# Down projections of four feed-forward layers as seven half-size products, woven into the next up projection, with one PSUM pool

## The chip, the cores and the metric

The kernel runs on one NeuronCore of a Trainium2 chip. Its engines work side by side, each through an order of instructions that is fixed when the kernel is built: TensorE (PE) multiplies, VectorE (DVE), ScalarE (ACT) and GpSimd (POOL) do the elementwise work, and SyncE (SP) issues nearly all loads. An engine starts its next instruction when the semaphores that this instruction waits for are up; the ones behind it wait with it. The metric is the device time of one execution in microseconds.

## What is computed

Two transformer blocks of two layers each run over 512 tokens of width 1024, in fp32.

```python
# block one, layers 0 and 1
x = layer_norm(ALPHA * x + mixer(x), ...)            # l=0: HGRN2 recurrence + convolution; l=1: pooling mixer
x = layer_norm(ALPHA * x + memory_cross_attention(x, mem_n, wq, wk, wv, wo), ...)
x = layer_norm(ALPHA * x + swiglu_ffn(x, ffn_wg[l], ffn_wu[l], ffn_wd[l]), ...)
# block two: gated linear attention (layer 0), sliding-window attention (layer 1), and after each
x = x + sq_relu_mlp(rmsnorm(x, g), w_up[l], w_down[l])

def swiglu_ffn(x, w_gate, w_up, w_down):             # hidden width 2816
    return (jax.nn.silu(x @ w_gate) * (x @ w_up)) @ w_down

def sq_relu_mlp(h, w_up, w_down):                    # hidden width 4096
    u = jax.nn.relu(h @ w_up)
    return (u * u) @ w_down
```

## The kernel before

**Products.** A number is held as two fp32r parts, high and low (`split`: ACT writes the high part, line 152, and DVE the rest, line 153). `mm3` (lines 180 to 182) makes one product of three matmuls: high by high, high by low, low by high. Weights come through SP in pieces of 512 KB, two blocks of 128 rows by 512 columns (`chunk`, line 161), into `rawp`, and are split into `wp`.

**Layers.** The 512 tokens are four tiles `r[0]` to `r[3]` of 128 rows. A projection whose output must stand with features on the partitions is `lin_a`; one whose output stands by token is `lin_b`, and the last one of a sublayer is `lin_out`. A feed-forward layer goes through its hidden features in blocks: `ffn` in blocks of 1024, 1024 and 768, `mlp` in four of 1024. Each block first makes the hidden values (with gate and up projection, or with the up projection alone), and then its part of the down projection for all 1024 outputs, which `resid` adds to `r`. The last block's part is a `lin_out`.

**Hand-over between sublayers.** `lin_out` makes the output by halves of 512 columns and by token tiles. When a tile's second half is done, `tail` adds it to `r[t]`, normalises `r[t]` where the layer asks for it (DVE and POOL, lines 275 to 294), and `nxt` makes what the next sublayer needs: `next_split` transposes `r[t]` on TensorE (line 254) and splits the result; `next_unit` first scales `r[t]` by its root mean square (ACT line 454, POOL, ACT line 479, into `z`) and transposes `z`; `next_pool` multiplies with banded matrices. The order in `lin_out` is, as (half, tile):

```python
for half, t in ((0, 0), (0, 1), (1, 0), (1, 1), (0, 2), (0, 3), (1, 2), (1, 3)):
```

**What sets the order.** The program is written sublayer by sublayer. A scheduler builds each engine's order from it when the kernel is built: program order is the priority, weight loads are raised by `high_priority`, and an instruction that is not ready may be passed by later ones. Buffers of one pool and tag are handed out in program order. PSUM has eight banks: five in the pool `mm` (accumulators of projections, `bank`) and three in the pool `aux` (`xbank`: transposes, attention scores, running sums, recurrence states).

Of the kernel before, what the change touches and what calls it, by code (L numbers as in the profile page):

```python
# [21 lines left out]
D_FF = 2816  # L22
# [50 lines left out]
class Net:  # L73
    def __init__(self, tc, a, ctx):
        self.tc, self.nc, self.a = tc, tc.nc, a
        pool = lambda name, bufs, **kw: ctx.enter_context(tc.tile_pool(name=name, bufs=bufs, **kw))
        self.const = pool("const", 1)
        self.wp = pool("wp", 4)
        self.rawp = pool("rawp", 3)
        self.big = pool("big", 16)  # L80
        self.work = pool("work", 2)
        self.small = pool("small", 4)
        self.mm = pool("mm", 5, space=bass.MemoryType.PSUM)
        self.aux = pool("aux", 3, space=bass.MemoryType.PSUM)
# [45 lines left out]
        return bank  # L130

    def xbank(self, shape):
        return self.aux.tile(shape, F32, tag="aux", name=self.nm("aux"))

    def bload(self, dst, ap):
        self.nc.sync.dma_start(dst, ap.unsqueeze(0).broadcast_to(list(dst.shape)))
# [38 lines left out]
                units.append(u)  # L175
        return units

    def mm3(self, ps, lh, ll, rh, rl, start, stop):
        nc = self.nc
        nc.tensor.matmul(ps, lh, rh, start=start, stop=False)  # L180
        nc.tensor.matmul(ps, lh, rl, start=False, stop=False)  # L181
        nc.tensor.matmul(ps, ll, rh, start=False, stop=stop)  # L182

    def lin_a(self, xT, W, c0, evac, w=512, halves=False, width=512, **kw):
        units = kw.pop("units", None) or self.chunk(W, c0, w, **kw)
        nf = w // 128
        spans = [(0, width // 2), (width // 2, width)] if halves else [(0, width)]
        for t0, t1 in spans:
            ps = [self.bank([128, t1 - t0]) for _ in range(nf)]
            for k in range(8):  # L190
                u = units[k // 2]
                xh, xl = xT(k)
                for f in range(nf):
                    sl = slice(f * 128, f * 128 + 128)
                    self.mm3(ps[f], u[:, 0, k % 2, sl], u[:, 1, k % 2, sl],
                             xh[:, t0:t1], xl[:, t0:t1], k == 0, k == 7)
            for f in range(nf):
                evac(f, ps[f], t0, t1)

    def lin_out(self, xT, W, first, norm, nxt, k0=0, nk=8, between=None, aside=None):  # L200
# [12 lines left out]
        nxt, early = nxt if isinstance(nxt, tuple) else (nxt, None)  # L213
        ev = self.tail(512, first, norm, nxt)
        for half, t in ((0, 0), (0, 1), (1, 0), (1, 1), (0, 2), (0, 3), (1, 2), (1, 3)):
            if half == 0:
                p = ps[t] or self.bank([128, 512])
                self.mm_b([p], [t], xT, ua, range(split, nk), nk)
                self.resid(t, p, 0, first)
                if early:  # L220
                    early(t)
            else:
                p = self.bank([128, 512])
                self.mm_b([p], [t], xT, ub, range(nk), nk)
                ev(t, p)
# [67 lines left out]
        else:  # L293
            self.nc.vector.tensor_tensor(r, r, ps, ALU.add)  # L294

# [1 line left out]

    def hgrn_mixer(self):
        nc, a = self.nc, self.a
# [475 lines left out]
    def ffn(self, l, nxt, aside):  # L775
        nc, a = self.nc, self.a
        xT = self.pair_view(self.hi, self.lo)
        lg, lb = self.gains("ln_ffn", l)
        first = True
        for b0, bw in ((0, 1024), (1024, 1024), (2048, 768)):  # L780
            nch = -(-bw // 512)
            hh, hl = self.new_xT("hid", nch)
            for c in range(nch):
                w = min(512, bw - c * 512)
                sg = self.slot([128, 4, 512], name="sg")
                self.lin_a(xT, a["ffn_wg"][l], b0 + c * 512,
                           lambda f, ps, t0, t1: nc.scalar.activation(sg[:, f, t0:t1], ps, AF.Silu),
                           w=w, halves=(first and c == 0))

                def ev_up(f, ps, t0, t1):  # L790
                    s = sg[:, f, t0:t1]
                    nc.vector.tensor_tensor(s, s, ps, ALU.mult)
                    self.split(hh[c][:, f, t0:t1], hl[c][:, f, t0:t1], s)
                self.lin_a(xT, a["ffn_wu"][l], b0 + c * 512, ev_up, w=w)
            hT = self.pair_view(hh, hl)
            last = b0 + bw == D_FF
            kw = dict(k0=b0 // 128, nk=bw // 128)
            f0 = first
            if last:
                self.lin_out(hT, a["ffn_wd"][l], f0, (lg, lb), nxt, aside=aside, **kw)  # L800
            else:
                self.lin_b(hT, a["ffn_wd"][l], 0, lambda t, ps: self.resid(t, ps, 0, f0), **kw)
                self.lin_b(hT, a["ffn_wd"][l], 512, lambda t, ps: self.resid(t, ps, 512, f0), **kw)
            first = False


# [1 line left out]

    def gla_prepare(self):
        nc, a = self.nc, self.a  # L810
# [85 lines left out]
    def mlp(self, l, nxt):  # L896
        nc, a = self.nc, self.a
        xT = self.pair_view(self.hi, self.lo)
        for b in range(4):
            hh, hl = self.new_xT("hid")  # L900
            for c in range(2):
                def ev_up(f, ps, t0, t1):
                    u = self.tmp()[:, :t1 - t0]
                    nc.scalar.activation(u, ps, AF.Relu)
                    nc.vector.tensor_tensor(u, u, u, ALU.mult)
                    self.split(hh[c][:, f, t0:t1], hl[c][:, f, t0:t1], u)
                self.lin_a(xT, a["w_up_2"][l], b * 1024 + c * 512, ev_up, halves=(b == 0 and c == 0),
                           gain=self.gain(2 + l))
            hT = self.pair_view(hh, hl)
            kw = dict(k0=b * 8, nk=8)  # L910
            if b == 3:
                self.lin_out(hT, a["w_down_2"][l], False, None, nxt, **kw)
            else:
                self.lin_b(hT, a["w_down_2"][l], 0, lambda t, ps: self.resid(t, ps, 0), **kw)
                self.lin_b(hT, a["w_down_2"][l], 512, lambda t, ps: self.resid(t, ps, 512), **kw)

    def rel_bias(self):
        nc, a = self.nc, self.a
# [204 lines left out]
```

## Time and profile before

| | |
|---|---|
| time, median of three runs | 2504.81 us (2504.08 to 2505.48) |
| span of the profiled execution | 2503.4 us |
| TensorE busy | 2458.3 us (98%) |
| VectorE busy | 1249.7 us (50%) |
| ScalarE busy | 944.6 us (38%) |
| GpSimd busy | 181.3 us (7%) |
| moved by DMA | 239.48 MB, 96 GB/s on the mean |

The profiled execution's span is 1.4 us below the median of the runs; sums are made on the span. Busy shares are means over the whole span; a stage's own limit is read from its window. The clock that TensorE was granted is shown as PEclk, where 1.00 is 2.4 GHz and 0.50 is 1.2 GHz.

### The profile page before, as it was taken

The page shows a single profiled execution, that of the slowest core. Times are in us where ns is not written, and L with a number is a line of the kernel's source. Part 1 is how long each engine was busy: PE and PEld are TensorE (multiplying, and loading weights), DVE is VectorE, ACT ScalarE, POOL GpSimd, SP SyncE. Part 2 cuts the span into 40 slices and gives each one's busy share as a digit, 9 for nine tenths or more (in the row PEclk, how much of TensorE's full clock was granted, in tenths as well). Part 3 has the DMA queues.
Part 4 walks back from the last instruction along what each step waited for, and adds up shares of the span by engine and source line. Part 5 has one row for each costly group of instructions (what it writes and reads, how often), then busy time and mean ns, then how long its engine had stood idle before and what let it go on. Part 6 is the DMA issues. An engine that isn't in the chain of part 4 may idle for free.

```text
span 2503.4 us, 30298 instructions
## 1 busy us (share of the span) xinstructions
PE 2458.3 (98%) x12334; PEld 2052.4 (82%) x12334; DVE 1249.7 (50%) x1772; ACT 944.6 (38%) x1576; POOL 181.3 (7%) x219
## 2 busy tenths in 40 slices
PE   8989999999999999999999999999999999999998
PEld 8876787888888997888888786888888877888887
DVE  4798566433326766433327423444444467444443
ACT  3643343222223343322224634433223456423323
POOL 1151300000000100000001003100000100000000
PEclk9999899999999999999999999999999999999999
DMA  6323122333324332233223223233222421222222
GB/s 214 109 102 102 53 85 77 92 99 95 99 74 144 123 130 76 85 101 99 95 76 121 69 85 43 76 101 101 93 101 98 142 74 51 72 97 95 99 93 84
DMA packets 121788, 239.48 MB, mean 96 GB/s; under 512 B 7849, under 2 KB 14309, under 8 KB 121392
## 3 DMA queue, kind: packets, MB, share of 16 engines
q1 hardware_dynamic: 118976, 229.73, 28.3%
q0 software_dynamic: 2096, 6.76, 1.4%
q8 instruction: 97, 1.59, 0.3%
q10 hardware_dynamic: 576, 1.05, 0.1%
q14 instruction: 43, 0.35, 0.0%
HBM read 234.34 MB, written 6.32 MB: 96 GB/s over the span
## 4 chain that ended last, share of the span: by engine, by line
PE 90%; DVE 6%; issue 1%; ACT 1%; DMA 1%; POOL 0%; SPq 0%; POOLq 0%; DVEq 0%; ACTq 0%
PE mm L180 28%; PE mm L181 27%; PE mm L182 27%; DVE acc L525 2%; PE aux L254 2%; PE aux L581 1%; DVE w L153 1%; PE aux L180 1%; PE mm L608 1%; PE mm L605 1%; PE aux L182 1%; PE aux L181 1%; DVE bn L275 0%; PE aux L1043 0%; DMA raw<-in_ffn_wg 0%
## 5 line engine op out<-in xcount | busy, mean ns | idle before, releaser
L153 DVE TENSOR_TENSOR w<-raw,w 128x1024 fp32r<-128x1024 f32 (+1 forms) x286 | 341.0, 1195 | 604.4 <-ACT w L152 604.1
L181 PE MATMUL mm<-xTl,w 128*128 128x512 f32 (+1 forms) x1696 | 614.0, 363 | 2.2 <-DVE xTl L153 2.2
L180 PE MATMUL mm<-xTh,w 128*128 128x512 f32 (+1 forms) x1696 | 610.4, 363 | 1.0 <-ACT w L152 0.8
L182 PE MATMUL mm<-xTh,w 128*128 128x512 f32 (+1 forms) x1696 | 605.7, 362 | 0.0
L152 ACT ACTIVATE w<-raw 128x1024 fp32r<-128x1024 f32 (+1 forms) x286 | 293.8, 1029 | 748.8 <-PE mm L182 598.3
L181 PEld LDWEIGHTS mm<-xTl,w 128*128 128x128 f32 x1696 | 321.5, 190 | 50.8 <-DVE xTl L153 2.4
L180 PEld LDWEIGHTS mm<-xTh,w 128*128 128x128 f32 x1696 | 320.9, 190 | 50.4 <-ACT w L152 1.2
L182 PEld LDWEIGHTS mm<-xTh,w 128*128 128x128 f32 x1696 | 319.4, 189 | 48.8
L181 PE MATMUL mm<-w,hidh 128*128 128x512 f32 x752 | 292.0, 389 | 0.0
L180 PE MATMUL mm<-w,hidh 128*128 128x512 f32 x752 | 291.1, 389 | 0.0
L182 PE MATMUL mm<-w,hidl 128*128 128x512 f32 x752 | 288.9, 389 | 0.0
L173 DVE SCALAR_TENSOR_TENSOR w<-raw,gains_T,w 128x512 fp32r<-128x512 f32 (+1 forms) x200 | 139.0, 738 | 212.0 <-ACT w L172 211.3
L172 ACT ACTIVATE w<-raw,gains_T 128x512 fp32r<-128x512 f32 (+1 forms) x200 | 131.3, 707 | 237.3 <-PE mm L182 220.9
L182 PEld LDWEIGHTS mm<-w,hidl 128*128 128x128 f32 x752 | 141.2, 188 | 29.3
L180 PEld LDWEIGHTS mm<-w,hidh 128*128 128x128 f32 x752 | 141.2, 188 | 29.2
L181 PEld LDWEIGHTS mm<-w,hidh 128*128 128x128 f32 x752 | 141.2, 188 | 29.1
L180 PE MATMUL mm<-w,xTh 128*128 128x512 f32 (+1 forms) x352 | 135.1, 386 | 0.0
L181 PE MATMUL mm<-w,xTh 128*128 128x512 f32 (+1 forms) x352 | 135.1, 384 | 0.0
L182 PE MATMUL mm<-w,xTl 128*128 128x512 f32 (+1 forms) x352 | 134.8, 384 | 0.0
L294 DVE TENSOR_TENSOR r<-r,mm 128x512 f32<-128x512 f32 x112 | 76.3, 686 | 72.8 <-PE mm L182 72.7
L525 DVE SCALAR_TENSOR_TENSOR acc<-u,pack,acc 128x511 f32<-128x511 f32 (+29 forms) x90 | 83.7, 972 | 0.0
L180 PEld LDWEIGHTS mm<-w,xTh 128*128 128x128 f32 x352 | 66.5, 189 | 15.5 <-issue 2.3
(323 smaller groups left out, 3344.9 us busy)
## 6 DMA issues: line engine op xcount, KB each, us to landing
raw<-in_w_up SPq DMA_DIRECT2D x64, 512.0 KB, 3.6
raw<-in_w_down SPq DMA_DIRECT2D x64, 512.0 KB, 3.2
raw<-in_ffn_wd SPq DMA_DIRECT2D x44, 512.0 KB, 3.2
raw<-in_ffn_wg SPq DMA_DIRECT2D x40, 512.0 KB, 3.6
raw<-in_ffn_wu SPq DMA_DIRECT2D x40, 512.0 KB, 3.5
raw<-in_ab_w_in SPq DMA_DIRECT2D x24, 512.0 KB, 3.8
raw<-in_a_w_in SPq DMA_DIRECT2D x24, 512.0 KB, 3.6
raw<-in_xa_wk SPq DMA_DIRECT2D x16, 512.0 KB, 3.3
```

The lines of the kernel that those rows point to most:

```text
L152: self.nc.scalar.activation(hi, src, AF.Copy)
L153: self.nc.vector.tensor_tensor(lo, src, hi.bitcast(F32), ALU.subtract)
L172: nc.scalar.activation(u[:, 0, i], raw[:, i], AF.Identity, scale=g)
L173: nc.vector.scalar_tensor_tensor(u[:, 1, i], raw[:, i], g, u[:, 0, i].bitcast(F32), ALU.mult, ALU.subtract)
L180: nc.tensor.matmul(ps, lh, rh, start=start, stop=False)
L181: nc.tensor.matmul(ps, lh, rl, start=False, stop=False)
L182: nc.tensor.matmul(ps, ll, rh, start=False, stop=stop)
L254: self.nc.tensor.transpose(ps[:, j, :], src[:, j * 128:j * 128 + 128], self.ident)
L294: self.nc.vector.tensor_tensor(r, r, ps, ALU.add)
L525: nc.vector.scalar_tensor_tensor(dst, src, col, dst, ALU.mult, ALU.add)
L581: nc.tensor.matmul(d[:, h - h0, :], ke[rows, t, h * 128:h * 128 + 128], vh(t, h)[rows, :], start=True, stop=True)
L605: nc.tensor.matmul(o, P[:, h, :], vh(t, h), start=True, stop=False)
```

## The change

**Down projections.** In each feed-forward layer, the down projection of every block but the last is made by `down_steps`. It cuts a product of 512 tokens by 1024 hidden features by 1024 outputs into halves in all three directions and makes seven products of half size instead of eight, after Strassen and Winograd: sums and differences of the hidden blocks (`s1`, `s2`) and of the weight blocks (`chain`) go into products that share accumulators (`x`, `y`, `z`, two banks each). There are two such blocks in each of two `ffn` layers and three in each of two `mlp` layers, ten in all.

**Order of the work.** `down_steps` and the hidden projections of the next block (`hidden`, `lin_steps`) are generators. `weave` takes one product and then two steps (`ffn`) or one step (`mlp`) of the other in turn.

**Pools.** The two PSUM pools become one of eight banks, `xbank` takes from it too, `rawp` grows from 3 to 5 and `big` shrinks from 16 to 15.

```diff
-        self.rawp = pool("rawp", 3)
-        self.big = pool("big", 16)
+        self.rawp = pool("rawp", 5)
+        self.big = pool("big", 15)
-        self.mm = pool("mm", 5, space=bass.MemoryType.PSUM)
-        self.aux = pool("aux", 3, space=bass.MemoryType.PSUM)
+        self.mm = pool("mm", 8, space=bass.MemoryType.PSUM)
     def xbank(self, shape):
-        return self.aux.tile(shape, F32, tag="aux", name=self.nm("aux"))
+        return self.mm.tile(shape, F32, tag="mm", name=self.nm("aux"))
+    def weave(self, main, side, per):
+        main, side = iter(main), iter(side)
+        for _ in main:
+            for _ in range(per):
+                next(side, None)
+        for _ in side:
+            pass
+    def down_steps(self, h, W, k0, first, ahead=120):
...
+        def product(d, us, banks, start):
+            for t in range(2):
+                tk = slice(t * 128, t * 128 + 128)
+                for k in range(4):
+                    u = us[k // 2]
+                    self.mm3(banks[t], d[:, 0, k, tk], d[:, 1, k, tk], u[:, 0, k % 2], u[:, 1, k % 2],
+                             start and k == 0, k == 3, skip_group_check=not start)
...
+        with early():
+            tt(s1, a21, a22, ALU.add)
+            d = left(s1)
+            us = []
+            for c, p, q in zip(halves(chain), block(0, 1), block(0, 0)):
+                tt(c, p, q, ALU.subtract)
+                us.append(self.wsplit(c))
+        z = pair()
+        product(d, us, z, True)
+        out(1, 1, z)
+        yield
...
     def mlp(self, l, nxt):
...
-            if b == 3:
-                self.lin_out(hT, a["w_down_2"][l], False, None, nxt, **kw)
-            else:
-                self.lin_b(hT, a["w_down_2"][l], 0, lambda t, ps: self.resid(t, ps, 0), **kw)
-                self.lin_b(hT, a["w_down_2"][l], 512, lambda t, ps: self.resid(t, ps, 512), **kw)
+        for b in range(1, 4):
+            more = []
+            out = self.new_xT("hid") if b == 3 else None
+            self.weave(self.down_steps(h, a["w_down_2"][l], 8 * b - 8, False), hidden(b, more, out), 1)
+            h = more
+        self.lin_out(self.pair_view(*out), a["w_down_2"][l], False, None, nxt, k0=24, nk=8)
```

Two places show what becomes of the order of TensorE's instructions. The first is the end of block one's layer 0 cross-attention: `xa_wo`'s second half for token tile 1 (before, its last rows for tile 3), the transposes of `r1` and `r2` (the rows with `consts`, the identity), and the next projection `ffn_wg` (`xTh`, `w`). In the kernel before:

```order
L181 MATMUL mm_485_3614<-wb_462_3405,oh_449_3350 128x512
L182 MATMUL mm_485_3614<-wb_462_3405,ol_450_3351 128x512
L254 MATMUL aux_477_3524<-consts_79,r1_88 128x128 x4
L254 MATMUL aux_478_3531<-consts_79,r1_88 128x128 x4
L254 MATMUL aux_483_3600<-consts_79,r2_110 128x128 x4
L180 MATMUL mm_506_3693<-xTh_463_3408,w_499_3675 128x256
L180 MATMUL mm_507_3694<-xTh_463_3408,w_499_3675 128x256
```

In the changed kernel, where `mm_473` is the second half of tile 1 and `mm_479` that of tile 2:

```order
L180 MATMUL mm_473_3485<-wb_462_3402,oh_449_3347 128x512
L181 MATMUL mm_473_3485<-wb_462_3402,ol_450_3348 128x512
L391 MATMUL aux_477_3521<-consts_76,r1_85 128x128 x4
L391 MATMUL aux_478_3528<-consts_76,r1_85 128x128 x4
L179 MATMUL mm_479_3561<-wb_456_3387,oh_429_3233 128x512
L180 MATMUL mm_479_3561<-wb_456_3387,oh_429_3233 128x512
```

Before, the transposes of tile 1 stood behind the products of all four tiles (`mm_485` is that of tile 3). Now they stand directly behind the product of tile 1, and the product of tile 2 stands behind them; tiles 2 and 3 follow in the same way.

The second place is the end of block one's layer 1: `ffn_wd`'s last block and the transposes of `z`, the scaled `r[0]`, for the gated linear attention. In the kernel before, `mm_1226` is the second half of tile 1, `mm_1235` and `mm_1236` are the first halves of tiles 2 and 3 (36 matmuls), and `mm_1237` is the second half of tile 2:

```order
L182 MATMUL mm_1226_9927<-wb_1207_9814,hidl_1149_9380 128x512
L180 MATMUL mm_1235_9978<-w_1197_9789,hidh_1146_9377 128x512
...
L182 MATMUL mm_1236_9998<-w_1201_9799,hidl_1149_9380 128x512
L180 MATMUL mm_1237_10018<-wb_1203_9804,hidh_1146_9377 128x512
L254 MATMUL aux_1224_9913<-consts_79,z_1222_9907 128x128 x4
L254 MATMUL aux_1225_9920<-consts_79,z_1222_9907 128x128 x4
L181 MATMUL mm_1237_10018<-wb_1203_9804,hidh_1146_9377 128x512
```

In the changed kernel, `mm_1293` is the second half of tile 0 and `mm_1302` that of tile 1:

```order
L180 MATMUL mm_1293_10005<-wb_1283_9943,hidh_1176_9206 128x512
L181 MATMUL mm_1293_10005<-wb_1283_9943,hidl_1178_9208 128x512
L391 MATMUL aux_1300_10042<-consts_76,z_1298_10036 128x128 x4
L391 MATMUL aux_1301_10049<-consts_76,z_1298_10036 128x128 x4
L179 MATMUL mm_1302_10056<-wb_1279_9933,hidh_1175_9205 128x512
L180 MATMUL mm_1302_10056<-wb_1279_9933,hidh_1175_9205 128x512
```

Before, the rest of tile 1 and 37 matmuls of tiles 2 and 3 stood between the end of tile 0's product and the transposes of its `z`; now none does.

## Rows read from the trace of the kernel before

**Rows 1.** The page: the span, and busy time by engine:
```profile
span 2503.4 us, 30298 instructions
...
PE 2458.3 (98%) x12334; PEld 2052.4 (82%) x12334; DVE 1249.7 (50%) x1772; ACT 944.6 (38%) x1576; POOL 181.3 (7%) x219
```

**Rows 2.** The weight loads' issues in SP's queue, start and length in us:
```profile
1672.16 40.11 SPq L161 DMA_DIRECT2D raw<-in_w_up  x8
...
1846.24 0.37 SPq L161 DMA_DIRECT2D raw<-in_w_up  x1
```

**Rows 3.** Busy us of each engine over two middle blocks of the first mlp:
```profile
1672.16:1846.24 174.08, 174.08 (x770) 144.20 (x769) 73.47 (x96) 55.80 (x80) 0.00 (x0) 1.00 0.30 97
```

**Rows 4.** Busy us in the first of nine hand-over windows, and the sum of all nine:
```profile
318.00:334.00 16.00, 13.53 (x100) 13.00 (x99) 11.40 (x16) 3.07 (x6) 3.52 (x4) 0.89 0.38 132
...
sum 317.00, PE 312.19 PEld 269.51 DVE 206.08 ACT 119.00 POOL 46.69; mean PE 34.69 PEld 29.95 DVE 22.90 ACT 13.22 POOL 5.19
```

**Rows 5.** Groups of DVE instructions by line and shape, mean ns of one:
```profile
L153 DVE TENSOR_TENSOR w<-raw,w 128x1024 fp32r<-128x1024 f32 x266 | 327.3, 1233 | 565.9 <-ACT w L152 565.7
...
L294 DVE TENSOR_TENSOR r<-r,mm 128x512 f32<-128x512 f32 x112 | 76.3, 686 | 72.8 <-PE mm L182 72.7
...
L905 DVE TENSOR_TENSOR tmp<-tmp 128x512 f32<-128x512 f32 x56 | 37.9, 691 | 25.3 <-ACT tmp L904 25.3
```

**Rows 6.** DVE in order of time after xa_wo, token tile 0:
```profile
427.16 0.69 DVE L292 SCALAR_TENSOR_TENSOR r<-r,mm 128x512 f32<-128x512 f32 x1 [3.19 <-PE mm L182]
427.88 0.69 DVE L275 BATCH_NORM_STATS2 bn<-r 128x6 f32<-128x512 f32 x1
428.61 0.21 DVE L277 BATCH_NORM_AGGREGATE mv<-bn 128x2 f32<-128x12 f32 x1
428.86 1.28 DVE L286 SCALAR_TENSOR_TENSOR r<-r,mv,w4k 128x1024 f32<-128x1024 f32 x1
430.92 1.29 DVE L287 SCALAR_TENSOR_TENSOR r<-r,rs,w4k 128x1024 f32<-128x1024 f32 x1 [0.78 <-POOL rs L269]
```

**Rows 7.** ACT in order of time after a_w_out_2, token tile 0:
```profile
1585.46 1.06 ACT L454 ACTIVATE z<-r 128x1024 f32<-128x1024 f32 x1 [5.16 <-DVE r L294]
1586.43 0.19 ACT L454 ACTIVATION_READ_ACCUMULATOR z<-r 128x1 f32 x1
1587.56 1.15 ACT L479 ACTIVATE z<-r,rs 128x1024 f32<-128x1024 f32 x1 [0.95 <-POOL rs L269]
```

**Rows 8.** POOL in order of time before a_w_out_2:
```profile
1559.63 4.82 POOL L885 TENSOR_TENSOR g<-g,w4k 128x512 f32<-128x512 f32 x3 [0.62 <-ACT g L883]
```

**Rows 9.** Busy us and clock (PEclk) in TensorE gaps and behind them:
```profile
128.50:131.80 3.30, 0.00 (x0) 0.00 (x0) 3.30 (x5) 1.24 (x2) 1.95 (x1) 1.00 0.17 40
131.90:136.00 4.10, 4.10 (x11) 3.21 (x12) 4.10 (x6) 0.22 (x2) 1.57 (x1) 0.58 0.23 86
141.20:144.20 3.00, 0.00 (x0) 0.00 (x0) 3.00 (x5) 1.08 (x2) 1.74 (x2) 1.00 0.19 72
144.30:152.00 7.70, 7.70 (x51) 7.70 (x52) 7.70 (x13) 2.55 (x3) 1.69 (x2) 0.78 0.20 69
195.98:197.56 1.58, 0.00 (x1) 0.00 (x0) 1.58 (x3) 1.06 (x1) 0.00 (x0) 1.00 0.00 0
197.60:201.70 4.10, 4.10 (x22) 3.16 (x22) 4.10 (x6) 0.00 (x0) 0.00 (x0) 1.00 0.48 135
320.20:322.40 2.20, 0.00 (x0) 0.00 (x0) 2.20 (x4) 0.00 (x0) 0.00 (x0) 1.00 0.68 238
322.40:330.00 7.60, 7.60 (x51) 7.60 (x52) 5.02 (x6) 0.58 (x2) 1.88 (x2) 0.78 0.26 93
2037.15:2039.10 1.95, 0.00 (x0) 0.02 (x1) 1.95 (x3) 0.93 (x2) 0.00 (x0) 1.00 0.00 0
2039.10:2047.00 7.90, 7.76 (x27) 5.81 (x28) 6.16 (x11) 2.67 (x9) 0.00 (x0) 0.57 0.22 69
```

More of the change, by code (lines that the diff above doesn't have):

```diff
@@ L176, in chunk, with mm3 @@
         return units
-    def mm3(self, ps, lh, ll, rh, rl, start, stop):
+    def mm3(self, ps, lh, ll, rh, rl, start, stop, **kw):
         nc = self.nc
-        nc.tensor.matmul(ps, lh, rh, start=start, stop=False)
-        nc.tensor.matmul(ps, lh, rl, start=False, stop=False)
-        nc.tensor.matmul(ps, ll, rh, start=False, stop=stop)
+        nc.tensor.matmul(ps, lh, rh, start=start, stop=False, **kw)
+        nc.tensor.matmul(ps, lh, rl, start=False, stop=False, **kw)
+        nc.tensor.matmul(ps, ll, rh, start=False, stop=stop, **kw)
     def lin_a(self, xT, W, c0, evac, w=512, halves=False, width=512, **kw):
@@ L198, in lin_a, with raw2, wsplit, lin_steps @@
                 evac(f, ps[f], t0, t1)
+    def raw2(self, W, k, c0):
+        raw = self.rawp.tile([128, 2, 512], F32, tag="raw", name=self.nm("raw"))
+        self.nc.sync.dma_start(
+            raw, W[k * 128:(k + 2) * 128, c0:c0 + 512].rearrange("(k p) c -> p k c", p=128))
+        return raw
+    def wsplit(self, src):
+        u = self.wp.tile([128, 2, 2, 512], F32R, tag="w", name=self.nm("w"))
+        self.split(u[:, 0], u[:, 1], src)
+        return u
+    def lin_steps(self, xT, W, c0, evac, w, gain=None, ahead=120):
+        ps, nf = None, w // 128
+        for k in range(0, 8, 2):
+            u, = self.chunk(W, c0, w, k, 2, ahead=ahead, gain=gain)
+            ps = ps or [self.bank([128, 512]) for _ in range(nf)]
+            for i in range(2):
+                xh, xl = xT(k + i)
+                for f in range(nf):
+                    sl = slice(f * 128, f * 128 + 128)
+                    self.mm3(ps[f], u[:, 0, i, sl], u[:, 1, i, sl], xh, xl, k + i == 0, k + i == 7)
+            if k == 6:
+                for f in range(nf):
+                    evac(f, ps[f], 0, 512)
+            yield
@@ new lines, in weave, with left, block, halves @@
+    def weave(self, main, side, per):
[6 more added lines that the diff above has]
+    def down_steps(self, h, W, k0, first, ahead=120):
+        nc = self.nc
+        early = lambda: self.tc.high_priority(offset=ahead)
+        lo, hi = slice(0, 256), slice(256, 512)
+        a11, a21, a12, a22 = h[0][:, :, lo], h[0][:, :, hi], h[1][:, :, lo], h[1][:, :, hi]
+        sums = self.slot([128, 2, 4, 256], name="sum")
+        s1, s2 = sums[:, 0], sums[:, 1]
+        chain = self.slot([128, 4, 512], name="chain")
+        tt = nc.vector.tensor_tensor
+        def left(src):
+            d = self.slot([128, 2, 4, 256], F32R, "A")
+            self.split(d[:, 0], d[:, 1], src)
+            return d
+        def block(i, j):
+            return [self.raw2(W, k0 + 4 * i + k, 512 * j) for k in (0, 2)]
+        def halves(t):
+            return [t[:, 0:2], t[:, 2:4]]
+        def product(d, us, banks, start):
[5 more added lines that the diff above has]
+                             start and k == 0, k == 3, skip_group_check=not start)
+        def out(i, j, banks):
+            for t in range(2):
+                self.resid(2 * i + t, banks[t], 512 * j, first and (i, j) not in done)
+            done.add((i, j))
+        done = set()
+        pair = lambda: [self.bank([128, 512]) for _ in range(2)]
+        with early():
+            d = left(a11)
+            us = [self.wsplit(b) for b in block(0, 0)]
+        x = pair()
+        product(d, us, x, True)
+        out(0, 0, x)
+        yield
+        with early():
+            d = left(a12)
+            us = [self.wsplit(b) for b in block(1, 0)]
+        y = pair()
+        product(d, us, y, True)
+        out(0, 0, y)
+        yield
+        with early():
+            tt(s1, a21, a22, ALU.add)
[7 more added lines that the diff above has]
+        out(1, 1, z)
+        yield
+        with early():
+            tt(s2, s1, a11, ALU.subtract)
+            d = left(s2)
+            us = []
+            for c, p in zip(halves(chain), block(1, 1)):
+                tt(c, p, c, ALU.subtract)
+                us.append(self.wsplit(c))
+        product(d, us, x, False)
+        out(0, 1, x)
+        yield
+        with early():
+            tt(a21, a11, a21, ALU.subtract)
+            d = left(a21)
+            us = []
+            for p, q in zip(block(1, 1), block(0, 1)):
+                tt(p, p, q, ALU.subtract)
+                us.append(self.wsplit(p))
+        product(d, us, x, False)
+        out(1, 1, x)
+        yield
+        with early():
+            tt(a12, a12, s2, ALU.subtract)
+            d = left(a12)
+            us = [self.wsplit(b) for b in block(1, 1)]
+        product(d, us, z, False)
+        out(0, 1, z)
+        yield
+        with early():
+            d = left(a22)
+            us = []
+            for c, p in zip(halves(chain), block(1, 0)):
+                tt(c, p, c, ALU.subtract)
+                us.append(self.wsplit(c))
+        product(d, us, x, False)
+        out(1, 0, x)
+        yield
@@ L778, in ffn, with hidden, ev_up @@
         lg, lb = self.gains("ln_ffn", l)
[L779 to L783, printed above, removed]
+        def hidden(b0, bw, to, split):
+            for c in range(-(-bw // 512)):
                 w = min(512, bw - c * 512)
                 sg = self.slot([128, 4, 512], name="sg")
[L786 to L790, printed above, removed]
+                to.append(sg)
+                silu = lambda f, ps, t0, t1, sg=sg: nc.scalar.activation(sg[:, f, t0:t1], ps, AF.Silu)
+                def ev_up(f, ps, t0, t1, sg=sg, c=c):
@@ L791, in ev_up @@
                     s = sg[:, f, t0:t1]
                     nc.vector.tensor_tensor(s, s, ps, ALU.mult)
[L793 to L800, printed above, removed]
-            else:
-                self.lin_b(hT, a["ffn_wd"][l], 0, lambda t, ps: self.resid(t, ps, 0, f0), **kw)
-                self.lin_b(hT, a["ffn_wd"][l], 512, lambda t, ps: self.resid(t, ps, 512, f0), **kw)
@@ L804, in ffn @@
-            first = False
+                    if split:
+                        self.split(split[0][c][:, f, t0:t1], split[1][c][:, f, t0:t1], s)
+                if b0 == 0 and c == 0:
+                    self.lin_a(xT, a["ffn_wg"][l], 0, silu, halves=True)
+                else:
+                    yield from self.lin_steps(xT, a["ffn_wg"][l], b0 + c * 512, silu, w)
+                yield from self.lin_steps(xT, a["ffn_wu"][l], b0 + c * 512, ev_up, w)
+        h = []
+        for _ in hidden(0, 1024, h, None):
+            pass
@@ L809, in gla_prepare @@
+        for b0, bw in ((1024, 1024), (2048, 768)):
+            more = []
+            out = self.new_xT("hid", 2) if bw < 1024 else None
+            self.weave(self.down_steps(h, a["ffn_wd"][l], (b0 - 1024) // 128, b0 == 1024),
+                       hidden(b0, bw, more, out), 2)
+            h = more
+        self.lin_out(self.pair_view(*out), a["ffn_wd"][l], False, (lg, lb), nxt, aside=aside, k0=16, nk=6)
     def gla_prepare(self):
@@ L898, in mlp, with hidden, ev_up @@
         xT = self.pair_view(self.hi, self.lo)
-        for b in range(4):
-            hh, hl = self.new_xT("hid")
+        W, g = a["w_up_2"][l], self.gain(2 + l)
+        def hidden(b, to, split):
             for c in range(2):
-                def ev_up(f, ps, t0, t1):
+                if not split:
+                    to.append(self.slot([128, 4, 512], name="h"))
+                def ev_up(f, ps, t0, t1, c=c):
                     u = self.tmp()[:, :t1 - t0]
                     nc.scalar.activation(u, ps, AF.Relu)
[L905 to L910, printed above, removed]
-            if b == 3:
-                self.lin_out(hT, a["w_down_2"][l], False, None, nxt, **kw)
-            else:
-                self.lin_b(hT, a["w_down_2"][l], 0, lambda t, ps: self.resid(t, ps, 0), **kw)
-                self.lin_b(hT, a["w_down_2"][l], 512, lambda t, ps: self.resid(t, ps, 512), **kw)
+                    if split:
+                        nc.vector.tensor_tensor(u, u, u, ALU.mult)
+                        self.split(split[0][c][:, f, t0:t1], split[1][c][:, f, t0:t1], u)
+                    else:
+                        nc.vector.tensor_tensor(to[c][:, f, t0:t1], u, u, ALU.mult)
+                if b == 0 and c == 0:
+                    self.lin_a(xT, W, 0, ev_up, halves=True, gain=g)
+                else:
+                    yield from self.lin_steps(xT, W, b * 1024 + c * 512, ev_up, 512, gain=g)
+        h = []
+        for _ in hidden(0, h, None):
+            pass
+        for b in range(1, 4):
+            more = []
+            out = self.new_xT("hid") if b == 3 else None
+            self.weave(self.down_steps(h, a["w_down_2"][l], 8 * b - 8, False), hidden(b, more, out), 1)
+            h = more
+        self.lin_out(self.pair_view(*out), a["w_down_2"][l], False, None, nxt, k0=24, nk=8)
     def rel_bias(self):
```

## The prediction

> **What bounds the kernel now.** The page comes first: TensorE is busy for 2458.3 of 2503.4 us [rows 1], so the other engines count only where TensorE waits for them, and a change pays only by fewer matmuls or costs only by new waits. Then the weight loads' issues, whose period is that of a block: two middle blocks of an `mlp` take 1846.24 - 1672.16 = 174.08 us [rows 2], and TensorE is busy for all of it [rows 3]. One such block is 2 x 192 = 384 matmuls of 512 columns (192 for the up projection, 192 for the down projection), so a matmul costs 87.04 / 384 = 0.2267 us when one follows another. DVE works 36.7 us of a block's 87. Last come the places where TensorE could wait and hardly does: nine windows in which one sublayer hands over to the next. Of their 317.0 us TensorE works 312.2 [rows 4], so 4.8 us are lost in all nine.
>
> **What the change removes.** A down projection's block becomes 7 products of 24 matmuls, 168 for 192. Ten blocks save 240 matmuls: 240 x 0.2267 = 54.4 us.
>
> **What it adds in the woven stretches.** Per block, by DVE's durations [rows 5]: 14 weight splits for 8 (+7.4 us at 1.233), 7 splits of hidden sums (8.6), 12 sums and differences of 128x1024 (which no row shows alone; a split reads as much, 1.233 each, 14.8), 14 additions to `r` for 8 (+4.1 at 0.686), less 8 splits of hidden values at the duration of a like operation (-5.5 at 0.691): +29.4, so 66 us of DVE in a block that TensorE now does in 81.6 us. The ten added loads of 512 KB bring a block to 26 x 0.52 MB in 81.6 us, 167 GB/s against 97 at a DMA share of 0.30 [rows 3]. Both fit under TensorE, and the steps of the up projection stand between two products, so I cost this at nothing. If the cover fails, the bound is the time of one split and one difference per product, 2.5 us x 70 products = 173 us; I take none of it, since DVE keeps a fifth of each block free and splits of the next product are raised ahead.
>
> **What the one pool moves.** This is the largest term, and it is not in the products at all. In the order of the changed kernel the transposes of a token tile stand directly behind that tile's product, since all PSUM buffers are now handed out from one row of eight in program order. TensorE can start nothing behind them. Before, other tiles' products and the next projection stood in between, and that is what covered the chain from a product to its transposes. Its length stays what it is:
>
> - With layer norm: DVE's addition to `r` starts at 427.16 and the second scaling ends at 430.92 + 1.29 = 432.21, so 5.05 us [rows 6].
> - With root mean square alone: an addition of 0.69, then ACT from 1585.46 to 1587.56 + 1.15 = 1588.71, so 3.95 us [rows 7].
> - With both (end of block one): 5.05 + 3.25 = 8.3 us.
>
> Counted through the changed order, with 12 or 17 matmuls (2.7 or 3.9 us) as cover where some still stand between:
>
> | hand-over | waits | us |
> |---|---|---|
> | `ab_w_out` to `xa_wq` | 3 x 5.05, one of 5.05 - 2.7 | 17.5 |
> | `xa_wo` to `ffn_wg`, layers 0 and 1 | 6 x 5.05, two of 5.05 - 3.9 | 32.7 |
> | `ffn` layer 0 to pooling | 4 x 5.05 | 20.2 |
> | pooling to `xa_wv` and `xa_wq` | 4 x 5.05 | 20.2 |
> | `ffn` layer 1 to linear attention | 4 x 8.3 | 33.2 |
> | linear attention to `mlp` 0 | 4 x 3.95 | 15.8 |
> | `mlp` 0 to window attention | 4 x 3.95 | 15.8 |
> | window attention to `mlp` 1 | 2 x 3.95, one of 3.95 - 2.7 | 9.1 |
>
> That is 164.5 us, less the 4.8 lost there now: 160 us, in 32 waits of 2 us or more. Queued behind each waiting transpose is TensorE's whole stream; DVE and ACT idle too once the chain is through.
>
> **The same inside the sublayers.** Softmaxes, running sums and recurrences were also covered by projections that stand elsewhere now. They are less regular, and I estimate. Each of four cross-attention softmaxes now has only its own scores beside it: about 5 us, 20 in all. In both recurrent mixers the gated outputs wait for POOL, which makes eight products of 128x512 at 4.82 / 3 = 1.6 us [rows 8], of which about 8 us end after the last matmul: 16 in all. Running sums and recurrences without filler: 13 in the first mixer, which waits there already now [rows 9], and 21 in the second. The convolution's norm, four tiles at 3: 12. Window attention: 15. Sum: 20 + 16 + 34 + 12 + 15 = 97 us. Bounds: 45 (about half, where some cover stays) and 150.
>
> **The clock.** After TensorE gaps of 3.3, 3.0, 2.2 and 1.95 us the granted clock falls: 0.58 over 4.1 us, 0.78 over 7.7, 0.78 over 7.6 and 0.57 over 7.9 [rows 9]. The time lost is 4.1 x 0.42 = 1.7, 1.7, 1.7 and 3.4 us. After a gap of 1.58 us it stays at 1.00. So each new wait of 2 us or more costs some 1.7 us beyond itself. With the 32 above and about 18 inside the sublayers: 50 x 1.7 = 85 us. Bounds: nothing (the fall lies inside a longer gap, when there is no work to slow down) and 126 (the mean of the four, 2.1 us, sixty times).
>
> The Trainium skill, "TensorE: Matmul & The Clock Gate", section "A second HAM failure mode: psum-queue depth-cycling", speaks against this change: a kernel that cycles through PSUM banks and so idles between groups of matmuls swings between the two clocks and loses throughput to the warming up between bursts. [...] The four gaps of this trace agree that the clock falls; they show 1.7 us lost behind a gap, not a burst.
>
> **Sum.** 2503.4 - 54.4 + 160 + 97 + 85 = 2791, and 1.4 for the way from the span to the runs' median: 2792, said as 2790.
>
> **Rivals.**
>
> - *The waits cost only themselves.* The clock falls inside the gaps and is back when work starts: 2503 - 54 + 160 + 97 = 2706 us. For it: the gaps are longer than those that the trace shows. Against it: the bursts between them, 24 matmuls or 5.4 us, are short.
> - *Bursts at half clock.* The clock falls in a gap and stays at 0.50 until the next one, so a 24-matmul burst (5.4 us) between two waits of 5 us takes 10.9 us. Each of some 32 bursts of 4 to 5.4 us then loses about 4.5 instead of 1.7: 2791 + 32 x 2.8 = 2880 us. Against it are the rows behind the gaps, where at most 3.4 us are lost [rows 9]. [...]
> - *DVE becomes the bound in the woven stretches.* Each product waits for a part of its split, some 0.7 of the 2.5 us above: 70 x 0.7 = 50, so 2840 us. For it: 66 of 81.6 us are spoken for, and the last block of an `mlp` also splits its hidden values. Against it: a block's loads and splits need no product of the same block.
> - *Faster, on the other side.* If the waits came out short, the 54.4 us would show: 2503 - 54 = 2450 us. It needs one thing, that a tile's chain is over when its transposes come up, and decides where a wait is under 54.4 / 50 = 1.1 us on the mean. The chains' 5.05 and 3.95 us stand against it [rows 6, 7], since no instruction of the chain is changed.
>
> **Numbers.** Forecast (2720 to 2860) 0.52; waits without the clock (2640 to 2720) 0.22; bursts at half clock 0.12; DVE bound 0.08; faster 0.04; the rest 0.02. The forecast is 2790. From 2650 to 2900 I leave out the faster case, the lower end of the case without the clock (145 for the waits, 45 inside the sublayers, 10 for the clock give 2650) and the upper end of the two slow ones (160 + 130 + 126 and 35 of DVE give 2902). A difference under 0.2%, 5 us, can't be told from no change here: faster 0.03, same 0.01, slower 0.96.
>
> **What would show it.** Right: after each hand-over's products the profile shows TensorE idle for 5 us (layer norm), 4 us (root mean square) or 8 us (both) with DVE, ACT or POOL as releaser, TensorE busy for about 2400 us plus what the slower clock adds, and PEclk under 1.00 in slices around the hand-overs but 1.00 in the woven stretches, where a middle `mlp` block takes 81.6 us between the same loads. Wrong: waits under 2 us at the transposes, or a woven block longer than 87 us, which would put the loss where I put none. The weakest term is the one inside the sublayers: it rests on estimates, and it could be half or half as much again.

## The result and the profile after

The changed kernel takes 2890.24 us (2889.5 us at the fastest) against 2504.9 us: a ratio of 1.1538, 95% interval 1.152 to 1.1556. One of its four runs took 9875.65 us, for which no profile here shows a reason, and the ratio leaves it out. The forecast was 2790 us with a range of 2650 to 2900. The direction and the mechanism were as forecast; the size was 100 us short. The time lies outside the band that the prediction held most likely (2720 to 2860, chance 0.52), and 10 us below the upper end of the range.

The page of the changed kernel, with the span, the busy time by engine, and the granted clock in 40 slices in tenths:

```profile
span 2887.7 us, 30332 instructions
...
PE 2554.9 (88%) x12094; PEld 2123.7 (74%) x12094; DVE 1529.3 (53%) x1994; ACT 1031.9 (36%) x1618; POOL 186.4 (6%) x219
...
PEclk9997889899998788999999798989999888899999
```

TensorE has 240 fewer matmuls, and yet it is busy for 96.6 us longer than in [rows 1], and idle for 332.8 us where it was for 45.1. So two things are to be found: 288 us of new idle time, and 96.6 + 54.4 = 151 us by which the matmuls that are left run longer.

The view of TensorE's waits by line and releaser (us in total, how often, the longest) finds the first:

```profile
PE aux L391 <- DVE r L424: 82.3, 16, 9.8
PE aux L391 <- ACT z L616: 78.8, 15, 9.8
PE aux L391 <- DVE tmp L831: 23.9, 12, 3.5
PE aux L1195 <- DVE s L1181: 20.9, 4, 6.8
PE mm L179 <- ACT w L151: 16.7, 8, 3.3
PE aux L581 <- DVE r L424: 15.5, 3, 5.2
PE aux L391 <- ACT qt L676: 15.0, 7, 9.4
...
PE aux L391 <- ACT tmp L538: 7.8, 2, 4.0
PE aux L707 <- ACT tmp L704: 6.7, 6, 1.8
PE aux L391 <- POOL qt L522: 6.5, 3, 4.7
...
PE aux L578 <- DVE r L424: 5.8, 1, 5.8
PE aux L391 <- POOL v L1030: 5.5, 3, 3.0
```

The four rows whose releaser is `r` (layer norm) or `z` (the root mean square's scaling) are the hand-overs: 82.3 + 78.8 + 15.5 + 5.8 = 182.4 us in 35 waits. One of them in DVE's order of time, at the place of the first order excerpt, with TensorE's transposes behind it:

```profile
520.76 0.69 DVE L429 SCALAR_TENSOR_TENSOR r<-r,mm 128x512 f32<-128x512 f32 x1 [3.73 <-PE mm L181]
521.48 0.69 DVE L412 BATCH_NORM_STATS2 bn<-r 128x6 f32<-128x512 f32 x1
522.21 0.21 DVE L414 BATCH_NORM_AGGREGATE mv<-bn 128x2 f32<-128x12 f32 x1
522.45 1.28 DVE L423 SCALAR_TENSOR_TENSOR r<-r,mv,w4k 128x1024 f32<-128x1024 f32 x1
524.50 1.28 DVE L424 SCALAR_TENSOR_TENSOR r<-r,rs,w4k 128x1024 f32<-128x1024 f32 x1 [0.76 <-POOL rs L406]
```

```profile
525.84 1.45 PE L391 MATMUL aux<-consts,r 128*128 128x128 f32 x6 [5.12 <-DVE r L424]
```

These are [rows 6] again, operation for operation. What was a chain beside other products is now a gap of 5.12 us. Most of the waits behind a layer norm are 5.12 or 5.21 us (forecast 5.05), those behind a root mean square 4.05 (3.95), those behind both 8.39 (8.3).

The second is the clock. Windows of the same hand-over (PE busy, then the other engines, then the clock in the third column from the end), the waits and the bursts in turn:

```profile
520.72:525.84 5.12, 0.00 (x1) 0.00 (x1) 4.16 (x5) 0.00 (x0) 1.80 (x2) 1.00 0.00 0
525.85:534.05 8.20, 8.20 (x32) 6.64 (x32) 1.38 (x2) 1.20 (x2) 0.00 (x0) 0.79 0.00 0
534.05:539.17 5.12, 0.01 (x2) 0.01 (x1) 4.16 (x5) 0.00 (x0) 1.80 (x2) 0.71 0.00 0
539.20:547.53 8.33, 8.33 (x32) 6.77 (x32) 1.38 (x2) 1.19 (x2) 0.00 (x0) 0.77 0.00 0
547.53:552.74 5.21, 0.00 (x1) 0.03 (x1) 4.16 (x5) 0.00 (x0) 1.80 (x2) 0.72 0.21 68
```

Here a burst loses 8.20 x 0.21 = 1.7 and 8.33 x 0.23 = 1.9 us, as [rows 9] had it, and part of the slow clock lies in the wait itself (0.71), where it costs nothing. Elsewhere it is worse. In the first mixer's recurrence, behind a wait before the pooling mixer, and in two stretches of the window attention:

```profile
218.80:259.80 41.00, 36.44 (x203) 26.17 (x202) 23.48 (x73) 7.81 (x29) 3.11 (x5) 0.50 0.08 30
...
905.30:917.87 12.57, 12.57 (x50) 11.15 (x50) 1.38 (x2) 1.19 (x2) 0.00 (x0) 0.61 0.01 1
...
2379.40:2399.90 20.50, 13.51 (x48) 10.32 (x47) 13.73 (x33) 11.90 (x40) 1.03 (x2) 0.50 0.00 0
2444.30:2464.80 20.50, 16.45 (x51) 12.11 (x52) 12.76 (x33) 11.96 (x39) 0.00 (x0) 0.50 0.14 49
```

In the recurrence TensorE runs for 41 us at 1.2 GHz though it is busy for 36.4 of them, with 203 mostly small matmuls.

The woven stretches of the `mlp` layers came out as costed. SP's queue gives the period of a block, and windows over the same two blocks DVE's share:

```profile
2006.79 7.01 SPq L201 DMA_DIRECT2D raw<-in_w_down  x4
...
2089.67 7.01 SPq L201 DMA_DIRECT2D raw<-in_w_down  x4
...
2171.86 0.46 SPq L201 DMA_DIRECT2D raw<-in_w_down  x1
```

```profile
2006.79:2089.67 82.88, 82.23 (x362) 67.42 (x361) 62.58 (x72) 36.44 (x46) 0.00 (x0) 1.00 0.50 165
2089.67:2171.86 82.19, 81.91 (x362) 67.50 (x361) 62.76 (x72) 36.42 (x46) 0.00 (x0) 1.00 0.50 166
```

A block takes 82.9 and 82.2 us where it took 87.04 [rows 2] (forecast 81.6), DVE works 62.7 of them (forecast 66), and 165 GB/s are moved (forecast 167). In the `ffn` layers one wait per block of products was not foreseen. In ACT's order of time:

```profile
674.60 1.96 ACT L922 ACTIVATE sg<-mm 128x512 f32<-128x512 f32 x3 [13.22 <-PE mm L181]
676.45 1.05 ACT L151 ACTIVATE A<-sum 128x1024 fp32r<-128x1024 f32 x1
677.39 0.59 ACT L922 ACTIVATE sg<-mm 128x512 f32<-128x512 f32 x1
677.87 1.06 ACT L151 ACTIVATE A<-sum 128x1024 fp32r<-128x1024 f32 x1
678.82 2.00 ACT L151 ACTIVATE w<-chain 128x1024 fp32r<-128x1024 f32 x2
```

ACT stands idle for 13.22 us on a SiLU that waits for the gate projection's last matmul, and the splits of the hidden sum `A` and of the weight difference `chain`, which the next product needs, are queued behind it. TensorE then waits 3.33 us, until 679.93, four times in all (13.3 of the 16.7 us of the row `mm L179 <- ACT w L151`). The window behind this wait shows the clock that it costs, 5.80 us of work at half clock, so about 2.9 us:

```profile
679.93:686.40 6.47, 5.80 (x13) 4.15 (x14) 6.47 (x7) 4.67 (x5) 0.00 (x0) 0.50 0.26 72
```

### The profile page after: what moved, and what is told of

It reads as the page before. It is cut to its first block, busy times and chain, and to the rows that moved or that the text cites. A ratio compares the mean times of both kernels' runs of the same rounds, so it can differ in the third digit from the quotient of the medians.

```text
span 2887.7 us, 30332 instructions
## 1 busy us (share of the span) xinstructions
PE 2554.9 (88%) x12094; PEld 2123.7 (74%) x12094; DVE 1529.3 (53%) x1994; ACT 1031.9 (36%) x1618; POOL 186.4 (6%) x219
## 4 chain that ended last, share of the span: by engine, by line
PE 68%; ACT 5%; DVE 4%; POOL 2%; issue 1%; DMA 1%; POOLq 0%; ACTq 0%; SPq 0%; DVEq 0%
PE mm L179 21%; PE mm L180 21%; PE mm L181 20%; PE aux L391 2%; DVE r L424 1%; ACT s L1173 1%; DVE r L431 1%; POOL rs L403 1%; ACT w L151 1%; ACT z L616 1%; DVE bn L412 1%; POOL rs L406 1%; ACT z L591 1%; PE aux L1195 1%; PE aux L581 1%
## 5 line engine op out<-in xcount | busy, mean ns | idle before, releaser
L179 PE MATMUL mm<-xTh,w 128*128 128x512 f32 (+1 forms) x1696 | 624.1, 368 | 3.8 <-ACT w L151 3.4
L180 PE MATMUL mm<-xTl,w 128*128 128x512 f32 (+1 forms) x1696 | 621.4, 366 | 0.0
L181 PE MATMUL mm<-xTh,w 128*128 128x512 f32 (+1 forms) x1696 | 604.6, 364 | 0.0
L151 ACT ACTIVATE w<-raw 128x1024 fp32r<-128x1024 f32 (+1 forms) x286 | 293.9, 1030 | 617.6 <-PE mm L181 538.5
L179 PEld LDWEIGHTS mm<-xTh,w 128*128 128x128 f32 x1696 | 327.4, 193 | 56.6 <-ACT w L151 6.0
L181 PEld LDWEIGHTS mm<-xTh,w 128*128 128x128 f32 x1696 | 324.4, 191 | 49.0
L179 PE MATMUL mm<-w,A 128*128 128x512 f32 x560 | 217.5, 395 | 15.0 <-ACT w L151 13.3
L180 PE MATMUL mm<-w,A 128*128 128x512 f32 x560 | 218.5, 392 | 0.0
L181 PE MATMUL mm<-w,A 128*128 128x512 f32 x560 | 214.9, 391 | 0.4 <-DVE A L152 0.4
L431 DVE TENSOR_TENSOR r<-r,mm 128x512 f32<-128x512 f32 x172 | 116.3, 683 | 160.9 <-PE mm L181 160.8
L179 PE MATMUL mm<-w,xTh 128*128 128x512 f32 (+1 forms) x352 | 137.1, 389 | 0.0
L179 PEld LDWEIGHTS mm<-w,A 128*128 128x128 f32 x560 | 105.9, 190 | 41.4 <-ACT w L151 15.0
L181 PEld LDWEIGHTS mm<-w,A 128*128 128x128 f32 x560 | 106.0, 189 | 22.9 <-DVE A L152 0.8
L180 PEld LDWEIGHTS mm<-w,A 128*128 128x128 f32 x560 | 106.2, 190 | 22.1
L391 PE MATMUL aux<-consts,r 128*128 128x128 f32 x160 | 36.1, 402 | 88.6 <-DVE r L424 82.3
L151 ACT ACTIVATE w<-chain 128x1024 fp32r<-128x1024 f32 x60 | 63.1, 1059 | 129.7 <-PE mm L181 85.6
```

Of the source, the lines that this page charges most:

```text
L151: self.nc.scalar.activation(hi, src, AF.Copy)
L179: nc.tensor.matmul(ps, lh, rh, start=start, stop=False, **kw)
L180: nc.tensor.matmul(ps, lh, rl, start=False, stop=False, **kw)
L181: nc.tensor.matmul(ps, ll, rh, start=False, stop=stop, **kw)
L391: self.nc.tensor.transpose(ps[:, j, :], src[:, j * 128:j * 128 + 128], self.ident)
```

## Experiments

All times are medians of timed runs, with their ratio to the kernel before in the same comparison.

**1. Only the pool.** The kernel before, with one edit:

```diff
-        self.mm = pool("mm", 5, space=bass.MemoryType.PSUM)
-        self.aux = pool("aux", 3, space=bass.MemoryType.PSUM)
+        self.mm = pool("mm", 8, space=bass.MemoryType.PSUM)
...
-        return self.aux.tile(shape, F32, tag="aux", name=self.nm("aux"))
+        return self.mm.tile(shape, F32, tag="mm", name=self.nm("aux"))
```

> The kernel before with one PSUM pool of eight banks for both uses, and nothing else. The one-pool theory: it has the changed kernel's waits without its saving, 2890 + 54 - 27 (the waits inside the woven ffn stretches) = about 2915 us. The rival that the products or the weaving cost the time: 2505 us, as before.

Measured: 2892.63 us, 1.1535 (1.1507 to 1.1562), 22 us less than expected. The pool alone makes the whole loss. Its longest rows of waits are those of the changed kernel:

```profile
PE aux L253 <- ACT z L478: 77.5, 15, 9.0
PE aux L253 <- DVE r L286: 77.1, 16, 9.7
```

That this run is hardly slower than the changed kernel (2.4 us) says that the seven products earned nearly nothing there. Beside each other, the changed kernel has 54.4 us less of matmuls, but 37 us more idle time (332.8 against 2893.0 - 2596.8 = 296.2 by the page below) and 12.5 us more of slow clock (2554.9 + 54.4 - 2596.8). Of the 37 us, 13.3 are the `ffn` waits; the rest was not followed up.

```profile
PE 2596.8 (90%) x12334; PEld 2166.0 (75%) x12334; DVE 1268.4 (44%) x1772; ACT 952.0 (33%) x1576; POOL 188.1 (7%) x219
```

**2. Only the products.** The changed kernel with the two pools back; `down_steps` takes three of its accumulators from `aux`:

```diff
-        self.mm = pool("mm", 8, space=bass.MemoryType.PSUM)
+        self.mm = pool("mm", 5, space=bass.MemoryType.PSUM)
+        self.aux = pool("aux", 3, space=bass.MemoryType.PSUM)
...
-        pair = lambda: [self.bank([128, 512]) for _ in range(2)]
+        pair = lambda: [self.xbank([128, 512]), self.bank([128, 512])]
...
-        x = pair()
+        x = [self.xbank([128, 512]) for _ in range(2)]
```

> The seven half-size products as in the changed kernel, but PSUM stays in two pools (mm 5, aux 3); x and one bank each of y and z come from aux. The one-pool theory: the transposes stand behind other tiles' products again, the hand-over waits and the slow clock behind them go, and the 54 us of the products show: 2504 - 54 = 2450, plus some 27 us if the four waits of 3.3 us per ffn layer pair and the slow clock behind them stay: 2450 to 2480 us. The rival, that the products, their splits or the weaving cost the time: 2750 us or more.

Measured: 2483.57 us, 0.9918 (0.9889 to 0.9948), 3.6 us above the expected range. The waits behind `r` and `z` are gone from the head of the list, and the four behind ACT's splits stand there:

```profile
PE aux L180 <- ACT w L152: 13.3, 4, 3.3
```

So the rival that the products, the splits or the weaving cost the time falls: with them, and without the one pool, the kernel is faster than before.

**3. The same pool, another place in the program.** The changed kernel with its one pool; `tail` writes the transposes of a tile one tile later:

```diff
-            nxt(t)
+            if t:
+                nxt(t - 1)
+            if t == 3:
+                nxt(3)
```

> The changed kernel with one pool, but the program writes a tile's transposes one tile later (tile 3's at the end). The theory that the order in which buffers are handed out, and so program order, makes the waits: a 24-matmul product (5.4 us) covers a chain of 5.05 us again, 32 hand-over waits fall to about 12, some 120 us of idle time and 50 to 70 us of slow clock go: 2690 to 2740 us. The rival, that one pool costs because its banks are too few or shared: 2890 us, no change.

Measured: 2712.42 us, 1.0826 (1.0799 to 1.0854), 178 us less than the changed kernel with the same eight banks. These 178 us come from the place in the row, not from the number of banks or their sharing, which are the same in both; the 208 us that are left above the kernel before, this run does not take apart. The waits behind `z` and `r` fall from 78.8 and 82.3 us to (13 waits, about 12 were expected):

```profile
PE aux L391 <- ACT z L619: 33.9, 7, 8.6
PE aux L391 <- DVE r L424: 28.4, 6, 6.7
```

**4. Only the hand-over.** The kernel before with its two pools, where the hand-over's buffers come from `mm`:

```diff
-    def transpose4(self, src):
-        ps = self.xbank([128, 4, 128])
+    def transpose4(self, src, bank=None):
+        ps = (bank or self.xbank)([128, 4, 128])
...
-                self.to_T(z[:, half * 512:half * 512 + 512], hi, lo, t, half)
+                self.to_T(z[:, half * 512:half * 512 + 512], hi, lo, t, half, self.bank)
...
-                ps = self.xbank([128, 4, 128])
+                ps = self.bank([128, 4, 128])
```

(and the same in `next_split`).

> The kernel before with its two pools (mm 5, aux 3), where only the hand-over's buffers (transposes of r and z, and the pooling mixer's band products) come from mm, in one row with the products' accumulators; softmaxes, running sums and recurrences stay in aux. The theory by parts: the hand-over waits of the changed kernel (182 us, less the 5 there now) and their slow clock (69 us by the run with filled waits), nothing inside the sublayers: 2505 + 177 + 69 = 2750 us. Rival: the waits come from sharing eight banks, not from the row they are handed out in: 2505 us.

Measured: 2780.47 us, 1.1102 (1.1084 to 1.1121). Five banks or eight, one row with the products is enough. Its page:

```profile
PE 2542.0 (91%) x12334; PEld 2117.1 (76%) x12334; DVE 1260.2 (45%) x1772; ACT 951.2 (34%) x1578; POOL 191.5 (7%) x219
```

With a span of 2778.4 us, TensorE is idle for 236.4 us, 191 more than before, and busy for 2542.0 - 2458.3 = 84 us more with the same matmuls. So the hand-overs cost 275 us, of which 84 are the clock; the expectation of 30 us less had too little new idle time (177 for 191) and too little clock (69 for 84). Of the idle time, 185 us stand in the rows behind `r` and `z`. Experiment 1 has 60 us more idle time than this run (296.2 - 236.4) and 55 us more of slow clock (2596.8 - 2542.0): that is roughly what one pool costs inside the sublayers.

**5. Waits filled.** The changed kernel, with matmuls on a constant in the waits, into a bank that nobody reads (28, 36 or 64 of them by the length of the chain). They are work beyond the reference's and leave its output as it is. The place where they are written:

```diff
+            if fill:
+                ps = self.xbank([128, 512])
+                for _ in range(fill):
+                    self.nc.tensor.matmul(ps[:, :256], self.steps[:, :128], self.steps, start=True, stop=True)
             nxt(t)
```

> The changed kernel (one pool) with TensorE kept busy in the hand-over waits: 28, 36 or 64 matmuls of 256 columns on a constant, into a bank that nobody reads, ahead of each tile's transposes. They add work and change no result. Theory that the clock falls because TensorE idles: the waits stay as long, but the clock stays at 1.00 behind them; 231 us of the 483 us at half clock lie there, so up to 116 us go: 2775 to 2810 us. Rival that the clock falls for another reason: 2890 us or a little more.

Measured: 2821.59 us, 1.1256 (1.1238 to 1.1275), 69 us less than the changed kernel. In the hand-over shown above, the filler takes most of the wait, 0.8 to 0.9 us of it stay, and the clock of the whole stretch is 1.00:

```profile
515.36 4.47 PE L557 MATMUL aux<-steps 128*128 128x256 f32 x36
```

```profile
520.64 1.09 PE L391 MATMUL aux<-consts,r 128*128 128x128 f32 x8 [0.82 <-DVE r L424]
```

```profile
510.00:560.00 50.00, 47.37 (x330) 43.93 (x329) 20.02 (x27) 7.65 (x15) 5.42 (x6) 1.00 0.13 43
```

Filler and rest together, 4.47 + 0.82 = 5.29 us, are no shorter than the wait of 5.12 us, so the gain lies behind it. Work that is of no use made the kernel faster, so in the hand-overs the clock does fall because TensorE idles. The gain is below the 80 to 116 us expected; that sum counted slow clock that lies inside the waits, too, which the windows above show to be free.

**6. Products without the weaving.** Experiment 2, with the seven products in a row and the up projection behind them:

```diff
-        main, side = iter(main), iter(side)
         for _ in main:
-            for _ in range(per):
-                next(side, None)
+            pass
         for _ in side:
             pass
```

> The two-pool version with all seven products in a row and the next up projection behind them. DVE then has some 7 us of work per product (two weight splits, one hidden split, sums, additions to r) against 5.4 us of TensorE. Theory that the weaving is the cover: 70 products x 1 to 1.7 us more, 2484 + 70 to 120 = 2555 to 2605 us, and slow clock beyond that where waits reach 2 us. Rival: DVE gets ahead during the up projection and the weaving is not needed: 2484 us.

Measured: 2606.26 us, 1.0395 (1.0378 to 1.0412), 123 us more than with the weaving. TensorE waits for DVE's splits and additions:

```profile
PE aux L181 <- DVE w L153: 44.8, 22, 5.0
PE aux L180 <- DVE r L430: 28.6, 10, 4.0
```

The cover that the prediction named for the 29 us of new DVE work per block is the up projection's steps, and this is its price.

**7. Sizes.** The kernel before with `rawp` 5 and `big` 15, and experiment 2 with 3 and 16:

```diff
-        self.rawp = pool("rawp", 3)
-        self.big = pool("big", 16)
+        self.rawp = pool("rawp", 5)
+        self.big = pool("big", 15)
```

> The kernel before with rawp 5 for 3 and big 15 for 16, and nothing else. All theories here: no change, 2505 us within 5. If one big buffer less made a wait, the time would go up by that wait.

Measured: 2510.03 us, 1.0015 (1.0005 to 1.0026), 4.6 us more.

> The two-pool version with rawp 3 and big 16, the sizes of the kernel before. If differences of two weight blocks need five raw buffers, loads are late and each block waits some microseconds: 2500 us or more. If the smaller big pool is what costs the 4.6 us seen in the run of the sizes alone: 2479 us.

Measured: 2508.99 us, 1.0013 (1.0003 to 1.0022), 25 us more than experiment 2. With the old sizes the saving of the products is gone. That the raw buffers do it, and not `big`, is not shown apart; one `big` buffer more is no likely reason for a loss. Nor is it waits, as the expectation had it: TensorE is idle for 73.8 us here and for 70.7 in experiment 2, but busy for 2427.8 us against 2410.5. Why the matmuls take longer stays open.

**8. The wait in the `ffn` layers.** Experiment 2 with one up step between two products in `ffn` as well:

```diff
-                       hidden(b0, bw, more, out), 2)
+                       hidden(b0, bw, more, out), 1)
```

> The two-pool version with one up step between two products in the ffn layers too, in place of two. Theory: in the two-pool run TensorE waits 3.33 us once per ffn block of products, since ACT's splits of the hidden sums stand in its queue behind SiLUs that wait for TensorE; the third product no longer follows the gate projection's end, so 4 x (3.33 + 3.4 of slow clock) = 27 us go if no new wait takes their place: 2457 us. Rival: the wait moves to another product behind a SiLU: 2475 to 2484 us.

Measured: 2459.59 us, 0.9815 (0.98 to 0.9829), the fastest version: 45.6 us under the kernel before, and 24 under experiment 2. Its page:

```profile
PE 2409.6 (98%) x12094; PEld 2009.8 (82%) x12094; DVE 1511.0 (62%) x1994; ACT 1028.2 (42%) x1620; POOL 180.2 (7%) x219
```

TensorE is busy for 48.7 us less than in [rows 1], of the 54.4 that the matmuls are worth. A window over the woven blocks of layer 0's `ffn`, in experiment 2 and then in this run:

```profile
450.00:730.00 280.00, 271.66 (x1231) 225.48 (x1230) 136.45 (x133) 86.09 (x97) 0.00 (x0) 0.98 0.40 125
```

```profile
450.00:730.00 280.00, 280.00 (x1307) 234.84 (x1306) 150.88 (x150) 95.50 (x107) 0.00 (x0) 1.00 0.43 133
```

The waits are gone there, and with them the slow clock. Over the whole kernel, though, the gain is all idle time: TensorE's busy time is nearly that of experiment 2 (2410.5 us) and the mean granted clock is 0.988 in both, since about as much half clock now stands in the first mixer and in the window attention. Why it moved there is not shown.

## Why the prediction was right, and where it was short

- **The saving.** 54.4 us: right. Experiment 8 shows 48.7 of them as busy time.
- **The woven stretches at nothing.** Right for `mlp` (82.2 to 82.9 us a block, at most 1.3 over the forecast). Wrong for `ffn`: 4 x 3.33 = 13.3 us of waits, and some 2.9 us of slow clock behind each, 12 in all. The step asked only whether DVE has time, and did not look at what is queued ahead of the splits on ACT. Experiment 8 gets 24 us back by moving it, near the sum of 25, but as a net figure.
- **The one pool.** Right, and the largest term as forecast. Experiments 1, 3 and 4 show the mechanism. Forecast 160 us of new idle time in hand-overs, measured 182.4 - 4.8 = 178. The chains were right to 0.2 us; the rest is in single waits. The waits forecast as partly covered (1.2 to 2.4 us) were 2.7 to 3.6 us, and two waits were 9.8 us: the first of those behind both norms, forecast at 8.3, and the last before `xa_wv`, forecast at 5.05. In the latter DVE puts three splits of the next weights (about 3.4 us) and a second addition and statistics (about 1.2) into the tile's chain. The splits in DVE's order, in TensorE's wait from 1033.56 to 1043.32:

```profile
1034.28 1.22 DVE L152 TENSOR_TENSOR w<-raw,w 128x1024 fp32r<-128x1024 f32 x1
...
1036.62 2.34 DVE L152 TENSOR_TENSOR w<-raw,w 128x1024 fp32r<-128x1024 f32 x2
```

- **Inside the sublayers.** Forecast 97 us of idle time; what is left of the 288 after hand-overs (178) and `ffn` (13) is 97. That the sum agrees is in part luck. By the list of waits above, the cross-attention softmaxes cost 23.9 us (forecast 20), the gated outputs behind POOL 6.5 + 5.5 (16), running sums and recurrences 15.0 + 6.7 and smaller rows (34), the convolution's norm 7.8 (12) and the window attention at least 20.9 (15). In experiment 1, without the products, the same places have only some 60 us more than experiment 4.
- **The clock.** This is the term that was mis-sized: forecast 85 us with an upper bound of 126, measured 151. Behind a wait of 5 us between bursts of 24 large matmuls, 1.7 us was about right in the hand-over shown, though of the prediction's own four gaps [rows 9] one had lost 3.4; windows over all 26 bursts between two waits of one hand-over give 2.2 us on the mean. It was too little in bursts with the pooling mixer's small matmuls (12.57 us at 0.61, so 4.9 us), and inside the sublayers, where recurrence and attention run long stretches at 0.50. By experiment 4 the hand-overs have 84 of the 151, where the prediction had 32 waits x 1.7 = 54; the `ffn` waits have about 12 by the window, where it had none; that leaves some 55 inside the sublayers, as between experiments 1 and 4, where it had 18 x 1.7 = 31. The rival of bursts at half clock gave 2880, near the time, but not by its mechanism: the 26 bursts are at 0.59 to 1.00, and none at 0.50.

Together: -54.4 + 178 + 97 + 13 + 151 = 384.6, against 2887.7 - 2503.4 = 384.3 us of span. This sum must come out, since the 97 and the 151 are what is left over of idle and busy time; what tests the parts are the experiments.

The Trainium skill, "TensorE: Matmul & The Clock Gate", section "A second HAM failure mode: psum-queue depth-cycling", tells of a kernel that idles between groups of matmuls as it cycles through PSUM banks, swings between the two clocks and loses throughput to this between its bursts. The changed kernel's trace agrees: it has 483 us at half clock in 61 stretches, against 39 us in 7 before, and filler alone gives back 69 us.

## What to carry to other kernels

When buffers of one pool go round in program order, a pool is also an order: put work that waits for a long chain (transposes after a norm or a softmax) into a pool of its own, or write it later in the program, or it stops the engine that should have covered it. Price a wait of TensorE with the clock that it costs behind it, and from windows of the kernel at hand: here it was 1.7 us in one hand-over and 4.9 in another. When new work is hidden under a saturated engine, look at every in-order queue that it passes through for an instruction ahead of it that waits.

## What the runs showed of the hardware beyond that

In the first mixer's recurrence the granted clock stood at 1.2 GHz for 41 us while TensorE was busy for 89% of the time, with 203 matmuls, most of them small. In the run with the filler, which leaves this place as it is, the stretch is still there (48 us); why it stays is not shown. In the gaps between large products, a constant's matmuls kept the clock at 2.4 GHz over the 50 us shown; over the whole kernel they left 249 us at half clock of 483.
